# Attention steps of 16 query columns with their own key window, and the retention scores of two heads in one step

## The chip, the cores and the metric

One core of one Trainium2 chip runs the kernel. The metric is the device time of one execution in microseconds (us); below, PE is TensorE, DVE is VectorE, ACT is ScalarE, POOL is GpSimd, and SP is the engine whose queue issues most DMAs.

## What is computed

Two layers of a diffusion backbone over 256 latent tokens (a grid of 4 rows by 64 columns) and 256 context tokens, 1024 wide. Each layer is a half-step SwiGLU FFN, a mixer, and another FFN. The mixer projects the tokens once and splits the columns into three groups of heads: neighbourhood attention (A), a spatial gate (B) and bidirectional retention (C). Attention and retention, cut to what matters here:

```python
# A: 6 heads x 64. Latent query (r, c) reads all 4 grid rows, 16 columns around c, and all context keys
col_start = jnp.clip(col - NA_WIN_C // 2, 0, GRID_W - NA_WIN_C)      # WIN_C 16, GRID_W 64
s_loc = jnp.einsum('bqhd,biqjhd->bhqij', q_r, k_win) * scale + bias
s_ctx = jnp.einsum('bqhd,bchd->bhqc', q_r, kc) * scale
p = jax.nn.softmax(concatenate([s_loc, s_ctx]))
out = p_loc @ v_win + p_ctx @ vc
# C: 6 heads x 64, per direction, chunks of 128
scores = jnp.einsum('bnihd,bnjhd->bnhij', qc, kc) * intra_decay
o = scores @ vc + cross_term(state)
y = norm(o_f) * silu(g_f) + norm(o_b) * silu(g_b)
```

In layer 0 the context tokens run through the mixer too; in layer 1 only the latent tokens leave it.

## The kernel before

Every large product (FFN, input and output projection) is done three times with operands split into a high and a low part in fp32r: `product` and `product_nat` (lines 204 to 217) issue three matmuls each. The weights come in chunks of 128x1024 through `Stream`: SP loads a chunk (`_load`, line 79), ACT rounds it to the high part (`wh`, line 89), DVE subtracts for the low part (`wl`, line 100). Three chunks are loaded and up to three are split ahead of PE.

Small work is put between these products by a queue written out by hand. After each product `pump` adds `pace[0]` (times the product's width over 512) to a counter, and for each whole unit it takes the next function, a tick, from the list `bg`. A tick whose condition isn't met yet (`needs`) stays where it is. `drain_bg` empties the list. So the order on every engine is fixed when the program is built, and an engine works through its own list in that order.

The mixer (`mixer`, from line 866) runs five stretches: `nat_group` three times for q, k, v of attention and v of retention (tokens on the partitions, evacuated by `ev0`, `ev1`, `ev2`), six projections `rqk` for q and k of retention, then gate groups, the spatial gate and the output projection. Attention ticks (`na_ticks`) begin in the third `nat_group` and go on beside `rqk`; retention ticks (`ret_ticks`) follow beside the gate groups.

An attention task is a pair of heads p and an index r. For r below 4 it takes one grid row of 64 queries: `na_scores` (line 992) multiplies them with all 256 latent and 256 context keys, one matmul of 512 columns for each head, the first head in rows and output partitions 0 to 63, the other in 64 to 127. DVE adds a bias tile (256 columns of bias, in which keys outside the window are -1e30, and 256 zeros) and takes the maximum, ACT the exponent, DVE the division; `na_pt` transposes four blocks of 128 keys, ACT copies them out, `na_pv` multiplies them with four blocks of values (`vN`). For r of 4 and 5, in layer 0 alone, the context queries read the context keys. There are 12 latent tasks a layer, and 6 context tasks in layer 0. A bias tile is loaded by SP two tasks ahead.

Retention, pair p: `ret_scores(p, e, s)` (line 1240) is one head e of one stream s (latent 0, context 1; in layer 1 only the latent one): two matmuls of 64 rows by 256 columns into one PSUM bank, and four DVE products with the decay tables into `sd`. `ret_o` (line 1259) multiplies them with the values into `ro`, and adds the term of the state at the second head; then `ret_ln`, `ret_var` and `ret_gate` (norm on DVE, ACT and POOL, gates on POOL) fill `yR`, which `yt` (line 1510) transposes for the output projection. All float32 matmuls of this part go through PE in two passes, so the profile counts two for each.

Small PSUM tiles come from two banks in turn (`a_bank`), `o` and `ro` from two others (`b_bank`).

Of the kernel before, what the change touches and what calls it, by code (L numbers as in the profile page):

```python
# [9 lines left out]
F32 = mybir.dt.float32  # L10
# [6 lines left out]
D = 1024  # L17
L = 2
# [8 lines left out]
GW = 64  # L27
NEG = -1.0e30
# [30 lines left out]
RPACE = (1.2, 1.4)  # L59
# [75 lines left out]
def tile_hybrid_dit(ctx: ExitStack, tc: tile.TileContext, t_x, t_c, t_cb, t_ada0, t_ada, t_adab, t_nw, t_w1, t_w2,  # L135
# [83 lines left out]
    with tc.manual_schedule():  # L219
# [219 lines left out]
        def residual(l, i, m, ps, c0, streams):  # L439
# [185 lines left out]
        def ffn(l, f, lead, norms, steps=None, tail=None):  # L625
# [7 lines left out]
            with ExitStack() as es:  # L633
# [21 lines left out]
                for half in range(2):  # L655
# [134 lines left out]
                    for m in range(KT - 2 if split_tail else KT):  # L790
# [10 lines left out]
                        if ahead and m >= KT - 2:  # L801
                            for s in seven.prepare(JH)[slice(0, 4) if m == KT - 2 else slice(4, 7)]:
                                s()
                        residual(l, i, m, ps, 0, streams)
                        if half == 1:
# [3 lines left out]
                            if tail:  # L809
                                tail(m)  # L810
# [55 lines left out]
        def mixer(l, norms):  # L866
            last = l == L - 1
            ctx_out = not last
            with ExitStack() as es:
# [9 lines left out]
                G.memset(biasT[:, :, 256:512], 0.0)  # L879
                btasks = [(p, r) for p in range(3) for r in range(4)]  # L880

                def bias_load(i):
                    if i < len(btasks):
                        SP.dma_start(out=biasT[:, i % 3, 0:256], in_=t_bias[l, btasks[i][0], btasks[i][1]])
# [7 lines left out]
                SP.dma_start(out=sgb, in_=t_sgb[l])  # L892

# [42 lines left out]
                na = {}  # L936
# [34 lines left out]
                def qk_transpose(tt, c, dst, w):  # L971
                    def go():
                        n = dst.shape[1]
                        ps = a_bank("qkt")
                        for p in range(n):
                            PE.transpose(ps[:, 128 * p:128 * p + 128], qkn[:, tt, c + 128 * p:c + 128 * p + 128], ident)
                        S.activation(out=dst[:, :, 128 * tt:128 * tt + 128],
# [13 lines left out]

                def na_scores(p, r):
                    def go():
                        ps = a_bank("sc")
                        for e in range(2):
                            h = slice(64 * e, 64 * e + 64)
                            PE.matmul(out=ps[h], lhsT=qT[h, p, 64 * r:64 * r + 64], rhs=kT[h, p, :],
                                      start=True, stop=True)
                        sc = mp.tile([128, 512], F32, tag="sc", name="sc", bufs=3)
                        mx = mp.tile([128, 1], F32, tag="mx", name="mx", bufs=3)  # L1000
                        V.tensor_tensor_reduce(out=sc, in0=ps, in1=biasT[:, (4 * p + r) % 3], scale=1.0,
                                               scalar=-3.0e38, op0=ALU.add, op1=ALU.max, accum_out=mx)
# [27 lines left out]
                def na_divide(p, r):  # L1030
                    def go():
# [3 lines left out]
                        for b in range(n):  # L1035
                            w = 512 // n
# [810 lines left out]
```

## Time and profile before

| what | value |
|---|---|
| median of three runs | 1810.83 us (1810.07 to 1811.4) |
| the profiled execution's own time | 1812.95 us |
| its span in the trace | 1811.2 us |
| PE busy | 1778.7 us, 98% |
| PEld (weight loads) busy | 1550.2 us, 86% |
| DVE busy | 1300.8 us, 72% |
| ACT busy | 724.8 us, 40% |
| POOL busy | 260.8 us, 14% |

The span is the time from the first to the last recorded instruction; about 1.8 us of the execution lie around it. Busy time of PE counts a matmul from its start to its modelled end, and neighbours overlap, so the distance between the starts of neighbours says more than their durations. In the timeline a row is: start, duration, engine, line, operation, output and inputs, form, count, and in brackets the idle time before it with the instruction that ended it. Without brackets, the engine had not been idle.

### The profile page before, as it was taken

How to read it: one execution, taken by the hardware profiler on the slowest of the kernel's cores; microseconds unless marked ns; L12 is line 12 of the kernel's file. 1: busy time of each engine (PE TensorE's matmuls, PEld its weight loads, DVE VectorE, ACT ScalarE, POOL GpSimd, SP SyncE). 2: the span in 40 equal slices, each digit the busy share in tenths (PEclk: the TensorE clock that was granted, in tenths of full speed). 3: DMA queues.
4: the chain of work that ended last, by engine and by line, in shares of the span. 5: the costliest groups of instructions: out<-in, count | busy, mean ns of one | idle time of the engine just before them, and what ended most of it. 6: DMA issues, size and time to landing. Idle time of an engine off the chain costs nothing. (4 is left out here: it accounts for less than half of the span.)

```text
span 1811.2 us, 29366 instructions
## 1 busy us (share of the span) xinstructions
PE 1778.7 (98%) x11520; PEld 1550.2 (86%) x11520; DVE 1300.8 (72%) x2200; ACT 724.8 (40%) x1203; POOL 260.8 (14%) x307
## 2 busy tenths in 40 slices
PE   7999999999999999999999999999999999999999
PEld 5788888888668989898999898979998867899998
DVE  5789988976455566788588877776887745668665
ACT  3422222225544234452344244513542555354443
POOL 0000000002114310120222002113311104310000
PEclk9999999999999999999999999999999999999999
DMA  8656765634211122656675526567666422356654
GB/s 316 236 190 217 252 212 189 212 124 149 87 64 47 47 74 67 174 147 188 179 183 158 164 86 179 153 210 199 169 188 222 146 88 76 106 192 200 200 179 148
DMA packets 103610, 290.60 MB, mean 160 GB/s; under 512 B 12080, under 2 KB 18864, under 8 KB 103344
## 3 DMA queue, kind: packets, MB, share of 16 engines
q1 hardware_dynamic: 86192, 243.64, 41.0%
q0 software_dynamic: 17280, 45.10, 10.8%
q8 instruction: 90, 1.47, 0.3%
q14 instruction: 48, 0.39, 0.1%
HBM read 287.64 MB, written 1.05 MB: 159 GB/s over the span
## 5 line engine op out<-in xcount | busy, mean ns | idle before, releaser
L100 DVE TENSOR_TENSOR wl<-wr,wh 128x1024 fp32r<-128x1024 f32 (+2 forms) x308 | 327.0, 1087 | 112.3 <-ACT wh L89 110.9
L89 ACT CAST wh<-wr 128x1024 fp32r<-128x1024 f32 (+2 forms) x308 | 279.9, 934 | 182.2 <-PE d L207 90.5
L208 PE MATMUL d<-aTh,wl 128*128 128x512 f32 (+1 forms) x770 | 269.6, 350 | 2.0 <-DVE wl L100 2.0
L206 PE MATMUL d<-aTh,wh 128*128 128x512 f32 (+1 forms) x770 | 269.9, 351 | 1.1 <-ACT wh L89 1.1
L207 PE MATMUL d<-aTl,wh 128*128 128x512 f32 (+1 forms) x770 | 269.2, 350 | 0.0
L208 PEld LDWEIGHTS d<-aTh,wl 128*128 128x128 f32 x770 | 145.3, 189 | 24.4 <-DVE wl L100 3.2
L206 PEld LDWEIGHTS d<-aTh,wh 128*128 128x128 f32 x770 | 145.2, 189 | 22.5 <-ACT wh L89 1.3
L290 DVE CUSTOM_DVE_ANT_0 aw<-aw,cb 128x1024 f32<-128x1024 f32 x128 | 155.6, 1223 | 11.5 <-DMA aw<-in_ada_dram 8.9
L207 PEld LDWEIGHTS d<-aTl,wh 128*128 128x128 f32 x770 | 145.3, 189 | 21.1
L206 PE MATMUL g<-hTh,wh 128*128 128x512 f32 (+2 forms) x464 | 158.1, 341 | 3.0 <-ACT hTh L383 1.4
L208 PE MATMUL g<-hTh,wl 128*128 128x512 f32 (+2 forms) x464 | 156.9, 338 | 2.0 <-DVE wl L100 1.9
L207 PE MATMUL g<-hTl,wh 128*128 128x512 f32 (+2 forms) x464 | 157.1, 339 | 1.3 <-DVE hTl L366 1.1
L208 PE MATMUL u<-hTh,wl 128*128 128x512 f32 (+2 forms) x464 | 156.6, 337 | 0.4 <-DVE wl L100 0.4
L206 PE MATMUL u<-hTh,wh 128*128 128x512 f32 (+2 forms) x464 | 156.1, 336 | 0.0
L207 PE MATMUL u<-hTl,wh 128*128 128x512 f32 (+2 forms) x464 | 156.0, 336 | 0.0
L214 PE MATMUL nat<-wh,hTh 128*128 128x512 f32 (+2 forms) x384 | 136.3, 355 | 0.0
L216 PE MATMUL nat<-wh,hTl 128*128 128x512 f32 (+2 forms) x384 | 127.9, 333 | 0.4 <-DVE hTl L366 0.4
L215 PE MATMUL nat<-wl,hTh 128*128 128x512 f32 (+2 forms) x384 | 127.7, 333 | 0.0
L290 DVE CUSTOM_DVE_ANT_0 junk<-aw,cb 128x1024 f32<-128x1024 f32 x96 | 117.0, 1219 | 4.5 <-DMA aw<-in_ada_dram 4.1
L582 PE MATMUL p<-hTh,wl 128*128 128x256 f32 x408 | 116.2, 285 | 0.6
L582 PE MATMUL p<-th,wl 128*128 128x256 f32 x408 | 114.8, 281 | 0.6 <-DVE wl L551 0.5
L581 PE MATMUL p<-hTl,wh 128*128 128x256 f32 x408 | 114.6, 281 | 0.0
(262 smaller groups left out, 4044.5 us busy)
## 6 DMA issues: line engine op xcount, KB each, us to landing
wr<-in_w_dram SPq DMA_DIRECT2D x142, 512.0 KB, 4.4
aw<-in_ada_dram SPq DMA_DIRECT2D x92, 512.0 KB, 5.1
wr<-in_wi_dram SPq DMA_DIRECT2D x56, 512.0 KB, 3.6
aw<-in_ada_dram POOLq DMA_DIRECT2D x52, 512.0 KB, 4.8
wr<-in_w_dram SPq DMA_DIRECT2D x64, 384.0 KB, 3.8
wr<-in_w_dram SPq DMA_DIRECT2D x64, 320.0 KB, 3.0
q<-in_w_dram SPq DMA_DIRECT2D x68, 256.0 KB, 3.8
q<-in_w_dram POOLq DMA_DIRECT2D x68, 256.0 KB, 5.3
```

Source lines behind the costliest of these rows:

```text
L89: self.nc.scalar.copy(out=h[:, :n], in_=self.raw[i][:, :n])
L100: self.nc.vector.tensor_tensor(out=lo[:, :n], in0=t[:, :n], in1=h[:, :n].bitcast(F32), op=ALU.subtract)
L206: PE.matmul(out=ps, lhsT=wh[:, col:col + 128], rhs=hh[rhs_sl], start=start, stop=False)
L207: PE.matmul(out=ps, lhsT=wh[:, col:col + 128], rhs=hl[rhs_sl], start=False, stop=False)
L208: PE.matmul(out=ps, lhsT=wl[:, col:col + 128], rhs=hh[rhs_sl], start=False, stop=stop)
L214: PE.matmul(out=ps, lhsT=hh[lhs_sl], rhs=wh[:, wc], start=start, stop=False)
L215: PE.matmul(out=ps, lhsT=hh[lhs_sl], rhs=wl[:, wc], start=False, stop=False)
L216: PE.matmul(out=ps, lhsT=hl[lhs_sl], rhs=wh[:, wc], start=False, stop=stop)
L290: V.tensor_tensor_reduce(out=junk, in0=t, in1=cb[:, s], scale=1.0, scalar=0.0, op0=ALU.mult, op1=ALU.add, accum_out=mod[l][:, 8 * r + b, s ...
L581: PE.matmul(out=ps, lhsT=wh[:, cw], rhs=tl, start=False, stop=False)
L582: PE.matmul(out=ps, lhsT=wl[:, cw], rhs=th, start=False, stop=n == 3)
```

## The change

The latent tokens are reordered (`POS`): within a chunk of 128 tokens, two grid rows by 64 columns, the two rows of a column now stand beside each other. An attention task r is now a block of 16 grid columns with all 4 rows, again 64 queries, and its keys are the 32 grid columns from `KB0[r]` on, again with all 4 rows: 128 latent keys instead of 256. Scores have 128 + 256 columns, in two matmuls a head; transposes and values go over three blocks instead of four. The values of the four windows are gathered into `vW` by eight copies within SBUF a call (`windows`), two calls in layer 0 and three in layer 1. `vN` now lives in the tile of `yR`. The first three bias tiles are loaded at the start of the mixer and each further one behind the task three before it; the table `tab` is issued ahead of the copies.

`ret_scores(p, s)` does both heads of a pair, alternating, into the two banks of `a_bank`. The scores of the next pair stand ahead of the last gate of the pair in front. `RPACE` goes from (1.2, 1.4) to (1.3, 1.5), the ticks of `evs` stand one further apart, and `ret_weights` moves back in the list. In the last FFN the result goes through a tile `xo`, which undoes the reordering in two DVE operations of 128 columns. Tables, bias and spatial weights are permuted on the way in.

```diff
+QB, KB = 16, 32
+KB0 = (0, 8, 24, 32)
...
-RPACE = (1.2, 1.4)
+RPACE = (1.3, 1.5)
...
-        def residual(l, i, m, ps, c0, streams):
+        def residual(l, i, m, ps, c0, streams, out=None):
+
+            if out is not None:
+                for k in range(2):
+                    a, b = 128 * k, 128 * k + 128
+                    V.scalar_tensor_tensor(out=out[:, a:b].rearrange("p (r c) -> p c r", r=2),
...
-                vN = mp.tile([128, 4, 384], F32, tag="vN", name="vN")
+
+                vW = mp.tile([128, 4, 384], F32, tag="vN", name="vW")
...
                 yR = mp.tile([128, 4, 384], F32, tag="yR", name="yR")
+                vN = yR
...
+                def windows(a, b):
+
+                    for w, c0 in enumerate(KB0):
+                        for c in range(2):
+                            SP.dma_start(out=vW[64 * c:64 * c + 64, w, a:b], in_=vN[2 * c0:2 * c0 + 64, c, a:b])
...
+                for b in range(3):
+                    bias_load(b)
...
                 def na_scores(p, r):
                     def go():
                         ps = a_bank("sc")
-                        for e in range(2):
-                            h = slice(64 * e, 64 * e + 64)
-                            PE.matmul(out=ps[h], lhsT=qT[h, p, 64 * r:64 * r + 64], rhs=kT[h, p, :],
-                                      start=True, stop=True)
-                        sc = mp.tile([128, 512], F32, tag="sc", name="sc", bufs=3)
+                        kw = kT[:, p, 0:T].rearrange("p (c i) -> p c i", c=2)[:, :, 2 * KB0[r]:2 * KB0[r] + 2 * KB]
+                        for out, rhs in ((ps[:, 128:384], kT[:, p, T:NT]), (ps[:, 0:128], kw)):
+                            for e in range(2):
+                                h = slice(64 * e, 64 * e + 64)
+                                PE.matmul(out=out[h], lhsT=qT[h, p, 64 * r:64 * r + 64], rhs=rhs[h],
+                                          start=True, stop=True)
+                        sc = mp.tile([128, 512], F32, tag="sc", name="sc", bufs=3)[:, 0:384]
...
-                        for b in range(4):
+                        for b in range(3 if r < 4 else 4):
                             PE.transpose(ps[:, 128 * b:128 * b + 128], sc[:, 128 * b:128 * b + 128], ident)
...
+                            vs, nq = (vW[:, r], vN[:, 2], vN[:, 3]), 64
+                            o = o[:, 0:T].rearrange("p (c w i) -> p c w i", c=2, w=4)[:, :, r]
...
-                def ret_scores(p, e, s):
+                def ret_scores(p, s):
+
                     def go():
-                        h = 2 * p + e
-                        hp = 64 * e
                         qk = rt["qk", p]
-                        ps = a_bank("rs")
+                        pse = [a_bank("rs") for e in range(2)]
                         for b in range(2):
-                            PE.matmul(out=ps[:, 256 * b:256 * b + 256],
-                                      lhsT=qk[hp:hp + 64, 1, s * T + 128 * b:s * T + 128 * b + 128],
-                                      rhs=qk[hp:hp + 64, 0, s * T:s * T + T], start=True, stop=True)
...
+                            for e in range(2):
+                                h = slice(64 * e, 64 * e + 64)
+                                PE.matmul(out=pse[e][:, 256 * b:256 * b + 256],
+                                          lhsT=qk[h, 1, s * T + 128 * b:s * T + 128 * b + 128],
+                                          rhs=qk[h, 0, s * T:s * T + T], start=True, stop=True)
...
-                    t = []
+
+                    t = [needs(0, ret_scores(0, 0))]
                     for p in range(3):
                         k = [needs(p + 1, f(p + 1)) for f in (ret_queries, ret_keys)] if p < 2 else [nop]
+                        ahead = [needs(p + 1, ret_scores(p + 1, 0))] if p < 2 else []
                         if ctx_out:
-                            t += [needs(p, ret_scores(p, 0, 0)), ret_scores(p, 1, 0), ret_o(p, 0, 0), ret_state(p),
-                                  ret_scores(p, 0, 1), ret_o(p, 1, 0), ret_ln(p, 0), ret_scores(p, 1, 1), *k,
-                                  ret_var(p, 0), ret_o(p, 0, 1), nop, ret_o(p, 1, 1), ret_ln(p, 1), nop,
-                                  ret_var(p, 1), ret_gate(p, 0), nop, nop, ret_gate(p, 1)]
+                            t += [nop, nop, ret_o(p, 0, 0), ret_state(p), nop,
+                                  ret_o(p, 1, 0), ret_scores(p, 1), ret_ln(p, 0), nop, ret_var(p, 0), nop,
+                                  ret_o(p, 0, 1), *k, nop, ret_o(p, 1, 1), ret_ln(p, 1), ret_gate(p, 0),
+                                  ret_var(p, 1), *ahead, nop, nop, ret_gate(p, 1)]
                         else:
...
+                            t += [nop, nop, ret_o(p, 0, 0), ret_state(p), *k,
+                                  ret_o(p, 1, 0), ret_ln(p, 0), nop, ret_var(p, 0), *ahead, nop, nop, ret_gate(p, 0)]
...
                 nat_group(full, lambda tt: (0, 512), ev0, stagger=True)
+                SP.dma_start(out=tab, in_=t_tab)
+                if last:
+                    windows(0, 128)
                 bg.extend(qk_ticks(0, full))
...
-                SP.dma_start(out=tab, in_=t_tab)
                 nat_group(full, lambda tt: (384, 512) if (last and tt >= 2) else (0, 512), ev1)
+                windows(128 if last else 0, 256)
...
                 nat_group(full, lambda tt: (0, 512), ev2)
+                windows(256, 384)
```

What PE issues in layer 0 around the first value step; `nat` are the projection's matmuls, `sc` scores, `pt` transposed weights, `o` the output. Before:

```order
L1046 MATMUL pt<-ident,sc 128x128 x4
L214 MATMUL nat<-wh,hTh 128x512
L215 MATMUL nat<-wl,hTh 128x512
L216 MATMUL nat<-wh,hTl 128x512
L976 MATMUL qkt<-ident,qkn 128x128 x2
...
L997 MATMUL sc<-qkT 64x512 x2
L1066 MATMUL o<-pt,vN 64x64 x8
```

And now:

```order
L1082 MATMUL pt<-ident,sc 128x128 x3
L217 MATMUL nat<-wh,hTh 128x512
L218 MATMUL nat<-wl,hTh 128x512
L219 MATMUL nat<-wh,hTl 128x512
L1003 MATMUL qkt<-ident,qkn 128x128 x2
...
L1033 MATMUL sc<-qkT 64x256 x2
L1033 MATMUL sc<-qkT 64x128 x2
L1111 MATMUL o<-pt,vW 64x2x32 x2
L1111 MATMUL o<-pt,yR 64x2x32 x4
```

The steps stand at the same places; they have three blocks for four, and the score step has two forms.

What PE issues for the last pair of layer 1; `rs` are the retention scores (with the numbers of their tiles), `ro` the outputs, `st` the state, `sg` the spatial gate, `yt` the transposes for the output projection. Before:

```order
L1247 MATMUL rs_14998<-rqk_14551 128x256 x2
...
L1247 MATMUL rs_15012<-rqk_14551 128x256 x2
...
L1275 MATMUL ro_15030<-rv_13397,sd_15001 128x64 x6
...
L1232 MATMUL st_15040<-vw_14875,kn_14873 128x256 x2
...
L1275 MATMUL ro_15030<-rv_13397,sd_15015 128x64 x6
L1283 MATMUL ro_15030<-st_bd_13402,prep_14536 128x128 x4
...
L1513 MATMUL yt_15144<-ident_74,yR_13398 128x128 x2
```

And now:

```order
L1288 MATMUL rs_14973<-rqk_14569 128x256
L1288 MATMUL rs_14974<-rqk_14569 128x256
L1288 MATMUL rs_14973<-rqk_14569 128x256
L1288 MATMUL rs_14974<-rqk_14569 128x256
...
L1413 MATMUL sg_14992<-sgw_13408,gvu_14698 64x128 x8
...
L1318 MATMUL ro_15036<-rv_13401,sd_14979 128x64 x6
...
L1318 MATMUL ro_15036<-rv_13401,sd_14984 128x64 x6
L1326 MATMUL ro_15036<-st_bd_13406,prep_14552 128x128 x4
...
L1563 MATMUL yt_15160<-ident_74,yR_13402 128x128 x2
```

Left out are projection matmuls (and the state). Between the last scores and the first `ro` there were 9 of them, now there are 27 and the eight of the spatial gate; between the last `ro` and the first `yt` there were 39, now 48. Each is 256 columns wide.

What SP issues in layer 1, from the weight loads of the first projection on (`wr`). Before:

```order
L79 DMA wr<-in_wi_dram 128x1024 x6
L1418 DMA tab<-in_tab_dram 128x1796
L79 DMA wr<-in_wi_dram 128x1024 x4
L884 DMA biasT<-in_bias_dram 128x256 x2
L79 DMA wr<-in_wi_dram 128x1024
```

And now:

```order
L904 DMA biasT<-in_bias_dram 128x128 x3
L82 DMA wr<-in_wi_dram 128x1024 x6
L1461 DMA tab<-in_tab_dram 128x1796
L910 DMA vW<-yR 64x128 x8
L82 DMA wr<-in_wi_dram 128x1024 x4
L910 DMA vW<-yR 64x128 x8
L82 DMA wr<-in_wi_dram 128x1024
L904 DMA biasT<-in_bias_dram 128x128 x2
```

Two groups of eight copies stand between weight loads that followed each other (the table's load apart), and a third stands further on, behind the third projection.

## Rows read from the trace of the kernel before

**Rows 1.** The page, busy time of each engine over the span, share and instructions.

```profile
PE 1778.7 (98%) x11520; PEld 1550.2 (86%) x11520; DVE 1300.8 (72%) x2200; ACT 724.8 (40%) x1203; POOL 260.8 (14%) x307
```

**Rows 2.** Windows of layer 0: us, then busy (instructions) by engine, PEclk, DMA share, GB/s.

```profile
457.00:483.00 26.00, 26.00 (x156) 16.86 (x158) 13.29 (x37) 11.67 (x24) 0.67 (x1) 1.00 0.25 81
555.00:600.00 45.00, 45.00 (x327) 40.41 (x325) 24.60 (x56) 14.13 (x29) 18.68 (x23) 1.00 0.16 48
```

**Rows 3.** Timeline of PE at one score step: start us, us, line, out<-in, forms, count.

```profile
456.33 0.39 PE L215 MATMUL nat<-wl,hTh 128*128 128x512 f32 x1
456.56 0.39 PE L216 MATMUL nat<-wh,hTl 128*128 128x512 f32 x1
456.88 1.07 PE L997 MATMUL sc<-qkT 64*64 64x512 f32 x4
...
458.46 0.40 PE L216 MATMUL nat<-wh,hTl 128*128 128x512 f32 x1
```

**Rows 4.** Timeline of PE at one transpose step, layer 0.

```profile
466.63 0.39 PE L216 MATMUL nat<-wh,hTl 128*128 128x512 f32 x1
466.87 0.60 PE L1046 MATMUL pt<-ident,sc 128*128 128x128 f32 x4
...
467.77 0.39 PE L216 MATMUL nat<-wh,hTl 128*128 128x512 f32 x1
```

**Rows 5.** Timeline of PE, a context score step and the value step behind it.

```profile
478.07 1.08 PE L1017 MATMUL sc<-qkT 64*64 64x256 f32 x8
479.08 0.69 PE L1066 MATMUL o<-pt,vN 128*64 128x64 f32 x16
```

**Rows 6.** Tile sc: duration of one pass, ns min/median/max, first and last start.

```profile
L997 PE MATMUL sc<-qkT x96: 589/614/641, 456.9 to 1508.3; 64*64 64x512 f32 x96
...
L1017 PE MATMUL sc<-qkT x48: 376/376/427, 478.1 to 541.1; 64*64 64x256 f32 x48
```

**Rows 7.** Timeline of PE at one retention score step of one head.

```profile
557.68 0.28 PE L215 MATMUL nat<-wl,hTh 128*128 128x256 f32 x1
557.80 0.28 PE L216 MATMUL nat<-wh,hTl 128*128 128x256 f32 x1
558.01 1.13 PE L1247 MATMUL rs<-rqk 64*128 64x256 f32 x4
...
559.41 0.28 PE L216 MATMUL nat<-wh,hTl 128*128 128x256 f32 x1
```

**Rows 8.** Timeline of PE, line 1275 undisturbed, and held in layer 0 and 1.

```profile
561.50 1.45 PE L1275 MATMUL ro<-rv,sd 128*128 128x64 f32 x12
...
612.24 1.83 PE L1275 MATMUL ro<-rv,sd 128*128 128x64 f32 x12 [0.66 <-DVE sd L1252]
...
1569.37 1.88 PE L1275 MATMUL ro<-rv,sd 128*128 128x64 f32 x12 [1.01 <-DVE sd L1252]
```

**Rows 9.** Window behind the last of these, columns as in rows 2.

```profile
1571.01:1574.42 3.41, 3.41 (x14) 3.05 (x14) 0.09 (x1) 0.57 (x3) 0.19 (x1) 0.50 0.00 0
```

**Rows 10.** Timeline of PE, the last transpose of the retention output, layer 1.

```profile
1587.12 0.44 PE L1513 MATMUL yt<-ident,yR 128*128 128x128 f32 x2 [2.52 <-POOL yR L1304]
```

**Rows 11.** DMA issues: tile, queue, count, KB each, median us to landing.

```profile
wr<-in_wi_dram SPq DMA_DIRECT2D x56, 512.0 KB, 3.6
...
tab<-in_tab_dram SPq DMA_DIRECT2D x2, 898.0 KB, 6.9
```

**Rows 12.** Timeline of SP and ACT in layer 1, around the table load.

```profile
1432.55 0.42 SPq L1418 DMA_DIRECT2D tab<-in_tab_dram  x1
1435.91 13.10 SPq L79 DMA_DIRECT2D wr<-in_wi_dram  x4
...
1446.36 1.04 ACT L89 CAST wh<-wr 128x1024 fp32r<-128x1024 f32 x1
```

**Rows 13.** Tile sd: a 128-column VectorE operation out of PSUM, ns.

```profile
L1253 DVE TENSOR_TENSOR sd<-rs,prep x18: 271/278/281, 559.5 to 1570.3; 128x128 f32<-128x128 f32 x18
```

**Rows 14.** Timeline of VectorE, the last residual of the run.

```profile
1807.62 0.48 DVE L441 SCALAR_TENSOR_TENSOR xT<-d,mod,xT 128x256 f32<-128x256 f32 x1 [2.90 <-PE d L208]
```

More of the change, by code (lines that the diff above doesn't have):

```diff
@@ L803, in ffn @@
                                 s()
+                        if tail and half == 1:
+                            o = fp.tile([128, T], F32, tag="xo", name="xo", bufs=4)
+                            residual(l, i, m, ps, 0, streams, o)
+                            tail(m, o)
+                            continue
                         residual(l, i, m, ps, 0, streams)
@@ L976, in go @@
                             PE.transpose(ps[:, 128 * p:128 * p + 128], qkn[:, tt, c + 128 * p:c + 128 * p + 128], ident)
+                        if w == 0 and tt < 2:
+                            S.activation(out=dst[:, :, 0:T].rearrange("p b (w c i) -> p b w c i", w=4, c=2)[:, :, :, tt],
+                                         in_=ps[:, 0:128 * n].rearrange("p (b w i) -> p b w i", b=n, w=4),
+                                         func=AF.Copy, scale=qkw[:, l, w:w + 1])
+                            return
                         S.activation(out=dst[:, :, 128 * tt:128 * tt + 128],
@@ L1048, in go @@
                         if r < 4:
-                            S.copy(out=pt, in_=ps)
+                            S.copy(out=pt[:, 0:384], in_=ps[:, 0:384])
                         else:
@@ L1090, in na_ticks @@
                     n = len(tasks)
-                    nb = [0]
+                    nb = [3]
                     def next_bias():
@@ L1742, in _tables @@
     sin = (np.sin(a) * np.where(d % 32 < 16, -1.0, 1.0)[:, None]).astype(f32)
[L1743 to L1744 removed]
+    sw = np.concatenate([128 + POS, POS])
+    dif = POS[None, :] - POS[:, None]
     df = np.concatenate([128 + dif, np.maximum(dif, 0)], 1)
@@ L1798, in _layout @@
     r["qkw"] = np.concatenate([qk, qk], 1).transpose(1, 0, 2)
-    bias = np.full((L, 3, 4, 2, GW, 4, GW), NEG, f32)
+    bias = np.full((L, 3, 4, 2, 2, QB, 2, 2, KB, 2), NEG, f32)
     col = np.arange(GW)
@@ L1806, in _layout @@
             for cq in range(GW):
+                w, c = divmod(cq, QB)
                 ck = np.arange(start[cq], start[cq] + WIN_C)
-                bias[:, :, r_, :, cq, kr, ck[0]:ck[-1] + 1] = rpb[:, :, :, kr - r_ + 7, ck - cq + WIN_C - 1]
-    r["bias"] = bias.reshape(L, 3, 4, 128, 256)
-    r["sgw"] = sg_w.transpose(0, 3, 1, 2)
-    r["sgb"] = np.repeat(sg_b.reshape(L, 2, 2, 128).transpose(0, 2, 1, 3), 64, axis=1)
+                bias[:, :, w, :, r_ // 2, c, r_ % 2, kr // 2, ck[0] - KB0[w]:ck[-1] + 1 - KB0[w], kr % 2] = (
+                    rpb[:, :, :, kr - r_ + 7, ck - cq + WIN_C - 1])
+    r["bias"] = bias.reshape(L, 3, 4, 128, 128)
+    r["sgw"] = sg_w[:, :, POS][:, :, :, POS].transpose(0, 3, 1, 2)
+    r["sgb"] = np.repeat(sg_b[:, :, POS].reshape(L, 2, 2, 128).transpose(0, 2, 1, 3), 64, axis=1)
     ln = np.stack([sg_ln_w, sg_ln_b], 1)
```

78 lines of the change are left out of this document (41 added, 37 removed).

## The prediction

> **What bounds the kernel now.** I read the page first, then windows, then the timeline of TensorE step by step. The page shows PE busy 1778.7 us of 1811.2, against 1300.8 on VectorE and 724.8 on ScalarE [rows 1]. A busy PE need not be at its peak, so the windows: while layer 0 does attention, PE has no idle time at all in 26 us, and VectorE and ScalarE are busy for only half of it; the same in its retention stage, 45.00 of 45.00 [rows 2]. So an instruction taken off PE there is time taken off the end, unless something new makes PE wait. What a small step costs is not its own duration but how far it pushes the projection matmuls apart. Between two neighbours of 512 columns lie 0.23 us, and 1.90 between 456.56 and 458.46 with one score step and two more neighbours between: the step costs 1.90 - 3 x 0.23 = 1.21 us [rows 3]. This is how I price every step.
>
> **Attention, 24 latent steps (12 a layer).** Each loses 128 of its 512 key columns. A 512-column pass lasts at least 589 ns, a 256-column pass 376, so a column is worth (589 - 376) / 256 = 0.83 ns; the two heads go side by side and float32 takes two passes, so 128 columns are 2 x 128 x 0.83 = 0.21 us [rows 6]. The step becomes eight instructions instead of four. That costs nothing: the context step has eight of 256 columns in 1.08 us, the same column count as the four of 512 in 1.07 [rows 3, 5]. Four transposes push the neighbours 1.14 - 0.69 = 0.45 us apart; one fewer saves 0.11 [rows 4]. Sixteen value passes take 0.69 us, of which I put down a third to entry and drain (the last pass of a context step, 0.376, is a third of that step's 1.08), so four fewer save 0.12; the ends are 0 and 4 x 0.69 / 16 = 0.17 [rows 5, 6]. Together 0.44 us, times 24 = **10.6 us**. The shorter maximum, exponent, divide and copy on VectorE and ScalarE run beside PE and count nothing.
>
> The two heads of a score step write halves of one PSUM bank, and the eight passes still fit into 1.08 us [rows 5]. The Trainium skill, TensorEngine Tiling (Array Packing), Restrictions and Gotchas, says that different row tiles cannot access the same bank at the same time; by that rule the heads would go one after the other, the column saving would double and the total would be 5 us lower. Here the trace differs from it, so I give it no chance.
>
> **Retention scores, 18 head steps become 9.** One head's step has four passes of 256 columns and costs 1.61 - 3 x 0.12 = 1.25 us [rows 7]. The four do not overlap: four take 1.13 us where eight paired ones of the same column count take 1.08 [rows 5, 7]. The change alternates the heads, which sit in the lower and the upper 64 rows of the array and go to two banks. No row of before shows that form (64 rows, all 128 output columns). The bounds are 1.20, a paired step that is no worse than attention's, and 1.25 + 4 x 0.25 = 2.25, no overlap at all, 0.25 being (1.13 - 0.376) / 3 a pass [rows 6, 7]. The nearest row is the paired one of 256 columns in float32, and I take 1.25: 18 x 1.25 - 9 x 1.25 = **11.3 us**.
>
> **Waits that go.** In the last pair of each layer the products of the scores (ro) waited for VectorE: 0.66 us and then 1.83 instead of 1.45 in layer 0, 1.01 and then 1.88 in layer 1, so 1.0 and 1.4 us [rows 8]. Behind the second the granted clock was 0.50 for 3.41 us, the 1.2 GHz level, which costs up to half of that, 1.7 us [rows 9]. Before, nine projection matmuls (1.06 us) lie in front of that ro in layer 1; in the new order 27 of them and the gating matmuls do, over 3.2 us, while VectorE needs four products of 0.28 to 0.42 us for a head [rows 13]. I take both waits as gone: **4.1 us**. The wait of the last transpose, 2.52 us, is for a chain (norm, POOL gate) that starts at the last ro; the new order puts nine more matmuls of 0.118 in between: **1.1 us** less, 1.4 stay [rows 10].
>
> **What it adds.** Five groups of eight copies within SBUF stand on SP's queue with weight loads behind them. The issue of a DMA takes 0.42 us, a group 3.4; in layer 1 the first group follows the table, which takes 6.9 us to land [rows 11, 12]. If the last copy waited for that, the load now issued at 1435.91 would leave at 1439.9. It lands 3.6 us later, at 1443.5, and its cast on ScalarE runs at 1446.36: covered, with 2.9 us left [rows 11, 12]. Were that cover gone, ScalarE's evacuations behind the cast would be late and PE with them. Between a group and the first value step that reads it stand over 6 us of projection matmuls and three attention steps in the new order, against 3.4 us of issue and 3.6 of landing. The last residual becomes two 128-column operations, 2 x 0.28 against 0.48: **+0.1 us** at the very end [rows 13, 14]. The bias loads move forward by less than a step; RPACE only spreads the queue of steps; both cost nothing while VectorE and ScalarE are half idle. With PE faster, one of nine joint steps may find VectorE late: I allow one wait of the size of the two above, **+1.2 us**.
>
> **Sum.** -10.6 - 11.3 - 4.1 - 1.1 + 0.1 + 1.2 = -25.8 us. Against the profiled execution, 1812.95, that gives 1787.2; the median of the three runs is 1810.83, 2.1 lower, so **1785.0 us**.
>
> **Rivals.** *A: the heads do not run side by side.* For it: no row shows this form; against it: float32 pairs in 64-row halves do in attention [rows 5]. A joint step then costs 2.25, the nine save 2.3 instead of 11.3, and the time is 1794.0. Between the ends it falls in between. (The Trainium skill, TensorE: Matmul & The Clock Gate, Part 3, measured 3.07x for four row tiles, 77% of the ideal; an estimate by that share stretches the paired passes from 1.0 to 1.3 us and gives 1787.7; no row here shows it.) *B: PE meets new waits in attention.* Steps come 0.44 us sooner, and the chain maximum, exponent, divide, transpose does not shrink as much. If half of the 24 steps give their gain back, 1790.3; all, 1795.6. Against it: VectorE and ScalarE are half idle there [rows 2]. *C, slower: SP holds the weights.* If the copies land one by one, a group holds SP for 8 x 3.6 = 29 us; the cover is 1446.36 - 1439.5 = 6.9 us, so five groups cost 5 x 22 = 110 us: 1895. It decides from 6.9 us a group on, and the kernel is slower than before from 12.8 (6.9 + 29.4 / 5). Against it: the load behind the table left 3.4 us after it, long before it landed [rows 11, 12].
>
> **Chances.** Forecast 0.78, A 0.11, B 0.08, C 0.03. The forecast's own range is 1780.5 (no wait returns, the last transpose's wait and the slow clock behind it go, 4.4 us lower) to 1788. The range reaches to A's end: 1780.5 to 1794. About 0.2% (3.6 us) is what a measurement of this kernel can tell from no change: faster 0.96, same 0.01, slower 0.03.
>
> **What would show it.** Score steps of eight passes that cost 1.0 us; three transposes at 0.33; joint retention steps of eight passes within about 1.1 us, starts in pairs (two more passes' worth each, and A is right); no ro row with a VectorE wait of 1 us in the last pair; one slow-clock stretch fewer; about 1.4 us before the last transpose. Wrong would be casts on ScalarE waiting for weight loads behind the copies (C), or transposes waiting for VectorE or ScalarE (B).

## The result, and the profile after

The median of four runs is 1793.32 us (1792.47 to 1796.28), against 1810.72 for the kernel before on the same chip: the ratio is 0.990, with a 95% interval of 0.9884 to 0.9915. The forecast was 1785.0 with a range of 1780.5 to 1794.0, so the direction held and the time lies just inside the upper end; the forecast's own range, without the rivals, ended at 1788. The profiled execution took 1793.33 us (span 1791.6), 19.6 less than that of before, where the sum said 25.8: 6.2 us of the miss of 8.3. The other 2.1 is the difference between before's profile (1812.95) and its median, which the profile after does not have.

The page, busy time by engine, answers to [rows 1]:

```profile
PE 1755.4 (98%) x11496; PEld 1544.3 (86%) x11496; DVE 1294.0 (72%) x2208; ACT 719.1 (40%) x1203; POOL 257.1 (14%) x307
```

PE lost 23 us of busy time and is still busy for 98% of the span. To see where the time went, the span is cut at the first product of each stage (`nat`, `su`, `op`, the next FFN), which stands at the same place in every kernel here. "Attention" runs from the first `nat` to the first gate group, "retention" from there to `op` (with `su`), "projection" to the FFN behind the mixer. All in us, from one profile each:

| kernel | L0 attention | L0 retention | L0 projection | L1 attention | L1 retention | L1 projection |
|---|---|---|---|---|---|---|
| before | 146.02 | 96.10 | 49.40 | 126.37 | 47.08 | 27.47 |
| after | 142.13 | 87.15 | 50.39 | 122.00 | 46.29 | 25.27 |
| e1, sg bank | 142.16 | 87.15 | 49.43 | 122.08 | 40.26 | 26.77 |
| e2, heads in turn | 142.17 | 87.19 | 50.37 | 122.01 | 46.15 | 25.27 |
| e3, attention alone | 142.09 | 96.13 | 49.40 | 121.35 | 47.09 | 27.46 |
| e4, retention alone | 145.99 | 87.14 | 50.38 | 126.98 | 46.47 | 26.78 |
| e5, copies twice | 142.11 | 87.15 | 50.38 | 126.88 | 46.38 | 26.76 |
| e6, weights back | 140.83 | 87.14 | 50.38 | 122.02 | 45.36 | 26.77 |
| e7, spacing back | 142.12 | 87.15 | 50.38 | 122.08 | 42.10 | 26.78 |
| e9, three edits | 140.84 | 87.14 | 49.42 | 121.98 | 40.27 | 25.22 |
| e11, gate later | 140.83 | 87.14 | 49.42 | 122.01 | 40.27 | 24.07 |
| e10, three tiles | 140.78 | 87.14 | 49.42 | 121.98 | 40.27 | 23.60 |

Stages with the same code agree within about 0.1 us from run to run, far better than the whole: the stretch ahead of the first mixer alone varies from 405.1 to 410.5 us, though no edit touches it. The exceptions are the last two columns, where a stretch at the lower clock comes or not: layer 1's retention takes 45.36 us in e6, with the granted clock at 0.50 for 3.41 us, and 46.29 in the change, with 6.83 us of it; for the projection see the last section. So the stages, read together with the clock, and not the medians, decide differences of a microsecond. From before to after the six columns sum to -19.2 us; the stretches outside them give -0.4.

**What came as forecast.** Timeline of PE in layer 0, a score step and a transpose step (start us, us, line, forms, count); answers to [rows 3, 4]:

```profile
454.88 0.40 PE L219 MATMUL nat<-wh,hTl 128*128 128x512 f32 x1
455.21 0.87 PE L1033 MATMUL sc<-qkT 64*64 64x256 f32 x8
...
456.57 0.39 PE L219 MATMUL nat<-wh,hTl 128*128 128x512 f32 x1
...
464.34 0.39 PE L219 MATMUL nat<-wh,hTl 128*128 128x512 f32 x1
464.57 0.49 PE L1082 MATMUL pt<-ident,sc 128*128 128x128 f32 x3
...
465.37 0.39 PE L219 MATMUL nat<-wh,hTl 128*128 128x512 f32 x1
```

By the reckoning of the prediction the score step costs 456.57 - 454.88 - 3 x 0.23 = 1.00 us (1.21 before), and the three transposes 465.37 - 464.34 - 3 x 0.23 = 0.34 (0.45 before).

Groups of instructions by line in the retention stage of layer 0, before (L1247) and after (L1288): busy us, mean ns of one, idle time ahead of it.

```profile
L1247 PE MATMUL rs<-rqk 64*128 64x256 f32 x48 | 13.5, 402 | 0.0
```

```profile
L1288 PE MATMUL rs<-rqk 64*128 64x256 f32 x48 | 6.8, 402 | 0.0
```

The same 48 passes of the same length cover half the time: they run two at a time.

**What did not.** Timeline of PE and VectorE in layer 1, from the last joint score step to the spatial gate's products `sg` (in brackets the idle time before, and what ended it):

```profile
1541.47 0.28 PE L219 MATMUL nat<-wh,hTl 128*128 128x256 f32 x1
1541.68 1.13 PE L1288 MATMUL rs<-rqk 64*128 64x256 f32 x8
...
1542.08 0.88 DVE L878 TENSOR_TENSOR gvu<-gvu,r 128x512 f32<-128x512 f32 x1 [0.24 <-POOL r L875]
...
1543.09 0.28 PE L219 MATMUL nat<-wh,hTl 128*128 128x256 f32 x1
...
1543.74 1.27 DVE L103 TENSOR_TENSOR wl<-wr,wh 128x1024 fp32r<-128x1024 f32 x1 [0.78 <-ACT wh L92]
...
1545.73 0.41 DVE L1294 TENSOR_TENSOR sd<-rs,prep 128x256 f32<-128x256 f32 x1
...
1546.46 0.41 DVE L1298 TENSOR_TENSOR sd<-rs,prep 128x256 f32<-128x256 f32 x1
...
1546.92 1.97 PE L1413 MATMUL sg<-sgw,gvu 128*64 128x128 f32 x16 [3.55 <-DVE sd L1298]
```

The joint step itself costs 1543.09 - 1541.47 - 3 x 0.118 = 1.27 us, as forecast. But `sg`'s operand `gvu` was written at 1542.96 and PE stood until 1546.9, until VectorE had finished the four products of the first head. `sg` reads nothing of those. What it shares with them is PSUM: it draws its bank from the pair of `a_bank`, and the joint step has just taken both. From 1545.56 on, still within the stall, the clock was at the 1.2 GHz level for 6.83 us (window of that stretch, columns as in [rows 2]):

```profile
1545.56:1552.39 6.83, 5.47 (x32) 5.14 (x33) 3.80 (x13) 0.55 (x1) 3.39 (x3) 0.50 0.23 77
```

Smaller waits, in the same view: the first value step of layer 0 with the VectorE and ScalarE work in front of it, `sg` of layer 0 with the `yt` whose bank it draws again and VectorE's reads of `yt`, the first `ro` of layer 1, and the last transpose, which answers to [rows 10]:

```profile
484.36 0.62 DVE L1185 TENSOR_SCALAR ww<-lg,tab 128x6 f32<-128x6 f32 x4
...
485.01 0.22 ACT L1187 ACTIVATE ww<-ww 128x24 f32<-128x24 f32 x1 [1.83 <-DVE ww L1185]
...
486.46 0.49 ACT L1085 COPY pt<-pt 128x384 f32<-128x384 f32 x1
...
487.00 0.34 PE L1111 MATMUL o<-pt,vW 128*64 128x64 f32 x4 [1.26 <-ACT pt L1085]
...
634.86 0.60 PE L1563 MATMUL yt<-ident,yR 128*128 128x128 f32 x4
...
639.47 1.40 DVE L1566 SCALAR_TENSOR_TENSOR hTl<-yt,gnw,hTh 128x512 fp32r<-128x512 f32 x2
...
640.27 1.09 PE L1413 MATMUL sg<-sgw,v 128*64 128x128 f32 x16 [0.89 <-DVE hTl L1566]
...
1509.04 1.83 PE L1318 MATMUL ro<-rv,sd 128*128 128x64 f32 x12 [0.21 <-DVE sd L1294]
...
1569.43 0.44 PE L1563 MATMUL yt<-ident,yR 128*128 128x128 f32 x2 [1.82 <-POOL yR L1347]
```

SP and ScalarE in layer 1 around the first group of copies, answers to [rows 12]; ahead of it the copies' own row from the view of tile `vW` (ns min/median/max of one issue):

```profile
L910 SPq DMA_DIRECT2D vW<-yR x40: 462/594/752, 450.5 to 1479.4; - x40
```

```profile
1420.69 0.42 SPq L1461 DMA_DIRECT2D tab<-in_tab_dram  x1
1421.16 8.11 SPq L910 DMA_DIRECT2D vW<-yR  x8
1429.37 7.78 SPq L82 DMA_DIRECT2D wr<-in_wi_dram  x4
...
1434.50 1.04 ACT L92 CAST wh<-wr 128x1024 fp32r<-128x1024 f32 x1
```

A group held SP for 8.1 us, not 3.4. Seven of its copies were issued at up to 0.75 us each by 1425.7; the eighth was issued at 1428.79, 0.02 us after the table had landed (8.1 us behind its issue at 1420.69). In the trace's records that copy waits for semaphore 104, the one that tells of the table's landing: the DMAs around the table take eight semaphores in turn, and the copy is the eighth behind it. The pause of 3.1 us is the case that the prediction named ("If the last copy waited for that"). The cast behind it ran at 1434.50; in the kernel before it ran at 1446.36, and this stage began 11.84 us later there (1408.56 against 1396.72), so it is not late at all.

### The profile page after: what moved, and what is told of

The parts are those of the page before. It is cut to its first block, busy times and chain, and to the rows that moved or that the text cites. A ratio compares the mean times of both kernels' runs of the same rounds, so it can differ in the third digit from the quotient of the medians.

```text
span 1791.6 us, 29394 instructions
## 1 busy us (share of the span) xinstructions
PE 1755.4 (98%) x11496; PEld 1544.3 (86%) x11496; DVE 1294.0 (72%) x2208; ACT 719.1 (40%) x1203; POOL 257.1 (14%) x307
```

## The experiments

**e1. A bank from the other pair for `sg`.**

```diff
                     def sg_mix(s):
...
-                        ps = a_bank("sg")
+                        ps = b_bank("sg")
```

> The changed kernel with one word altered: the spatial gate's products (sg) take their PSUM bank from the pair that ro and o use, not from the pair of which the joint retention scores now hold both. Bank theory: in layer 1 sg waited 3.55 us for the scores' products on VectorE to free a bank, though its operand was ready at 1542.96. It then starts at about 1543.2, the stretch of half clock behind it goes, and so does the wait of about 1 us in layer 0: sg falls from 5.88 and 2.19 us of displacement to 1.2 each, and the projection matmuls behind it lose their 1.5 us at half clock. Total 6 to 7 us less, about 1786.5. Rival, VectorE theory: it is VectorE that is late there, whatever the bank; then the first ro behind waits instead (sd is written at 1545.7 to 1547.9) and the total falls by less than 3 us, 1790 or more. Second rival, the operand: sg waits just as before, 1793.

Measured: 1787.99 us (1787.05 to 1788.43), ratio 0.987 (0.9855 to 0.9885). Timeline of PE and VectorE in layer 1 at the same place, and the last transpose; then the window behind that transpose:

```profile
1542.95 1.09 PE L1413 MATMUL sg<-sgw,gvu 128*64 128x128 f32 x16
...
1545.41 0.42 DVE L1294 TENSOR_TENSOR sd<-rs,prep 128x256 f32<-128x256 f32 x1
...
1546.94 1.45 PE L1318 MATMUL ro<-rv,sd 128*128 128x64 f32 x12
...
1563.05 0.44 PE L1563 MATMUL yt<-ident,yR 128*128 128x128 f32 x2 [1.83 <-POOL yR L1347]
```

```profile
1563.94:1567.35 3.41, 3.41 (x19) 3.41 (x18) 0.48 (x1) 0.99 (x2) 0.00 (x0) 0.50 0.02 5
```

`sg` now starts 2.5 us before VectorE touches the scores, with no wait, and the `ro` behind it has none either. The bank theory holds: layer 1's retention stage falls by 6.03 us and layer 0's projection by 0.96. (In layer 0 it is not a joint step that holds the bank: `sg` draws the bank of the first `yt`, 634.86, and VectorE read that `yt` only from 639.47 on.) VectorE is as late as before, only nobody needs it. The other 1.5 us went back: now the clock fell behind the last transpose, where in the change, with the same wait of 1.82 us, it had not.

**e2. The two heads in turn.**

```diff
-                        for b in range(2):
-                            for e in range(2):
+                        for e in range(2):
+                            for b in range(2):
```

> The changed kernel, where the joint retention step issues the four matmuls in the order head 0, head 0, head 1, head 1 and no longer in alternation; banks, products and order of steps are the same. If the saving comes from neighbours on different row halves that run side by side, only the passes at the change of head overlap: a joint step costs 2.0 to 2.25 us instead of 1.26, nine of them 6.7 to 9 us more, 1800 to 1802. If it comes from having one step instead of two (one entry and one drain of the queue instead of two), a step still costs about 1.26 and the time stays at 1793.

Measured: 1794.11 us (1790.11 to 1794.6), every stage as in the change. The order of issue did change; the order of one such step in the changed kernel and here, `rs_4728` and `rs_4729` being the two heads' banks:

```
-L1288 MATMUL rs_4728<-rqk_4165 128x256
-L1288 MATMUL rs_4729<-rqk_4165 128x256
-L1288 MATMUL rs_4728<-rqk_4165 128x256
-L1288 MATMUL rs_4729<-rqk_4165 128x256
+L1288 MATMUL rs_4728<-rqk_4165 128x256 x2
+L1288 MATMUL rs_4729<-rqk_4165 128x256 x2
```

Timeline of PE at that step, and a window of the first 0.1 us of it, `rs` alone (us, PE busy, passes in it, PEclk, DMA); then the same window at a one-head step of the kernel before:

```profile
1542.62 1.14 PE L1288 MATMUL rs<-rqk 64*128 64x256 f32 x8
```

```profile
1542.60:1542.70 0.10, 0.08 (x2) 1.00 0.69 246
```

```profile
1563.98:1564.08 0.10, 0.08 (x1) 1.00 0.59 246
```

The time fits the rival that expects about 1.26 us, but its reason does not: two passes are running in the first 0.1 us, although four of head 0 were issued ahead of the first of head 1. The halves run side by side, and they do so without being alternated. My first theory had the mechanism right and its condition wrong.

**e3 and e4. Each half alone.** e3 is the changed kernel with `ret_scores`, `ret_ticks`, RPACE and the spacing of before; e4 is the kernel before with those four of the change.

```diff
-RPACE = (1.3, 1.5)
+RPACE = (1.2, 1.4)
...
-                def ret_scores(p, s):
+                def ret_scores(p, e, s):
...
-                            at = min(at + 3, len(bg))
+                            at = min(at + 2, len(bg))
```

> The attention half of the change alone: scores per head, the retention steps' order, RPACE and the spatial gate's spacing are those of before. If the parts add up, 24 steps save 10.5 us, the wait of 1.3 us at the first value step of layer 0 stays, and the waits of ro and yt of before are back: 1801.5 us (1800 to 1803). If attention gives its gain back in new waits (the rival B of the prediction), 1806 or more.

> The retention half of the change alone, in the kernel before: joint scores, the new order of the retention steps, RPACE and the spacing of the spatial gate's steps. If the parts add up, 11.2 us less for the nine joint steps, about 4 less for the waits of ro that go, and about 7 more for the spatial gate that waits for a bank and the half clock behind it: 1802 to 1803. If the wait of the spatial gate is only there because the attention steps run ahead of VectorE, sg doesn't wait here and the time is 1796.

Measured: e3 1803.19 us (1801.47 to 1803.71), ratio 0.9953 (0.9938 to 0.9968); e4 1803.01 (1798.77 to 1805.47), ratio 0.9946 (0.9925 to 0.9966), both beside 1811.39 for before. That is -8.2 and -8.4, together -16.6 against -17.4 for the change: the halves add up. By the stages of the table they give 8.9 and 8.7 us, the change 19.2; 1.5 of the difference is the slow stretch in the last stage, which e4 has and the change has not. PE in layer 1 of e3 at the `ro` that waited in [rows 8], and `sg` in layer 1 of e4:

```profile
1559.04 1.83 PE L1315 MATMUL ro<-rv,sd 128*128 128x64 f32 x12 [1.02 <-DVE sd L1292]
```

```profile
1557.75 1.98 PE L1373 MATMUL sg<-sgw,gvu 128*64 128x128 f32 x16 [3.58 <-DVE sd L1258]
```

e3 keeps the old wait (1.02 us against 1.01); e4 has the new one, without any attention step running ahead. So the wait of `sg` belongs to the retention half alone.

**e5. Every copy twice.**

```diff
-                    for w, c0 in enumerate(KB0):
+                    for w, c0 in [*enumerate(KB0)] * 2:
```

> The changed kernel, where each of the five calls of windows issues its eight copies twice; nothing else. In the changed kernel a group holds the SP queue for 4.9 to 8.1 us in layer 1, more than the 3.4 of the prediction, and PE shows no wait behind one. If the cover was as wide as the prediction said (about 3 us past the first group), 5 to 8 us more of issue in each group uses it up in layer 1: the weight casts behind the groups start late and PE waits there, 1 to 4 us in all, 1794 to 1797. If the copies' transfers weigh on the other loads too (rival C), more than 10 us. If nothing on SP is near its edge, 1793.

Measured: 1798.79 us (1797.39 to 1802.05). Only layer 1's attention stage changed, by 4.88 us. SP, ScalarE and PE there:

```profile
1420.84 12.66 SPq L910 DMA_DIRECT2D vW<-yR  x16
1433.59 7.08 SPq L82 DMA_DIRECT2D wr<-in_wi_dram  x4
...
1438.01 1.04 ACT L92 CAST wh<-wr 128x1024 fp32r<-128x1024 f32 x1 [3.74 <-PE nat L218]
...
1440.20 0.50 PE L217 MATMUL nat<-wh,hTh 128*128 128x512 f32 x1 [2.15 <-ACT yR L959]
```

Counted from the start of the stage (1396.37 here, 1396.72 in the change), the load left 4.6 us later and landed 5.0 later (1437.91 against 1433.23). Its cast ran 0.10 us behind the landing, which ended its wait, and not the matmul that the bracket names; it ran 3.9 later than in the change. PE stood 2.15 us, was then 2.3 us later than in the change, and ran at half clock for 6.83 us (1441.11 to 1447.94). So the change had 1.2 us left between landing and cast and some 1.5 more at PE. Rival C is a real mechanism and begins between 8.1 and 12.7 us of hold for this group; at 12.7 it costs 4.9 us.

**e6. `ret_weights` at the head of the list again.**

```diff
-                t.insert(DEC[l][1], ret_weights)
...
-                bg.extend(t + ret_ticks())
+                bg.extend([ret_weights] + t + ret_ticks())
```

> The changed kernel with ret_weights back at the head of the list of steps, as before, and no longer in the sixth place of layer 0. If its four VectorE operations and ScalarE's exponent, which waited for them from 483.2 to 485.0, are what made the copy of the transposed weights late, the wait of 1.3 us at the first value step of layer 0 (487.00) shrinks to under 0.4 and the time falls by 1 us, to 1792. If the decay tables' exponents and the evacuations that stand there too make the copy late, the wait stays over 1 us and the time at 1793.

Measured: 1794.03 us (1792.32 to 1794.88), no gain that the medians show. The stage shows it: layer 0's attention is 1.30 us shorter than in the change. ScalarE and PE at the first value step:

```profile
488.96 0.50 ACT L1085 COPY pt<-pt 128x384 f32<-128x384 f32 x1
489.57 0.20 PEld L1111 LDWEIGHTS o<-pt,vW 128*64 128x64 f32 x4 [0.17 <-ACT pt L1085]
```

The copy comes 1.3 us after its transposes (487.65) where it came 2.7 after them (483.75) in the change. The cause is the four VectorE operations that ScalarE waited for. In this profile the stretches ahead of the mixer took 3.9 us more, and the slow clock behind the last transpose, which the change did not have, cost 1.5; both hide the gain in the total.

**e7. The spatial gate's steps two apart again.**

```diff
-                            at = min(at + 3, len(bg))
+                            at = min(at + 2, len(bg))
```

> The changed kernel with the spatial gate's steps two apart again, as before, in place of three. In layer 1 its products then stand 15 projection matmuls ahead of the last joint score step, where in the change they stand three behind it. By the bank theory the wait for the scores' products goes (VectorE's products come later than sg); sg may wait for its own norm instead, since its chain has 6 us less: up to 2 us. Total 3 to 6 us less in layer 1, about 1788 to 1790. If VectorE is simply overloaded there, the wait moves to sg's operand or to the next ro and the time stays above 1791.

Measured: 1789.98 us (1788.29 to 1790.69), ratio 0.988 (0.9852 to 0.9907). PE in layer 1:

```profile
1538.83 1.09 PE L1413 MATMUL sg<-sgw,gvu 128*64 128x128 f32 x16 [0.56 <-DVE gvu L878]
...
1546.69 1.83 PE L1318 MATMUL ro<-rv,sd 128*128 128x64 f32 x12 [0.70 <-DVE sd L1294]
```

With `sg` ahead of the joint step the 3.55 us are gone without another bank. It waits 0.56 for its own norm, and the `ro` 1.08 us in all (0.70 of idle and 0.38 more in its own duration, 1.83 against 1.45): 4.2 of e1's 6.0 us. The change's own move of `sg`, three apart instead of two, is what put it behind the joint step.

**e9, e11, e10. Towards a better version.** e9 takes e1 and e6 and, in layer 1, the last retention part last:

```diff
-                KORD = (0, 1, 2, 5, 6, 7, 3, 4)
+                KORD = (0, 1, 2, 5, 6, 3, 4, 7) if last else (0, 1, 2, 5, 6, 7, 3, 4)
...
-                for m in range(nm, 3):
-                    yt(m + 5)
+                if not last:
+                    for m in range(nm, 3):
+                        yt(m + 5)
                 for kt in KORD[3:6]:
+                    if kt == 3:
+                        yt(7)
```

> The changed kernel with the bank of the first experiment, ret_weights back at the head, and in layer 1 the last part of the retention output taken last: the output projection takes its inputs in the order 0, 1, 2, 5, 6, 3, 4, 7, and the last transpose (yt) stands 12 projection matmuls later. The wait of 2.0 us at yt falls to about 0.6, since 12 matmuls of 0.118 us stand in front of it now, and the stretch of half clock that the first experiment still had behind it goes (1.5 us). With the 5.3 us of the bank and 1 us of the weights: 1784 to 1785. If the products behind yt wait for its evacuation or for the spatial gate's split instead, 1786 to 1788.

Measured: 1786.24 us (1785.41 to 1787.13), ratio 0.9858 (0.9835 to 0.9881). The transpose no longer waits and no slow stretch follows, but the products that read the parts in front wait (the second case of the expectation). VectorE, ScalarE and PE there:

```profile
1560.63 0.69 DVE L1426 TENSOR_TENSOR gvu<-gvu 128x512 f32<-128x512 f32 x1
...
1561.35 0.62 ACT L1556 CAST hTh<-gvu 128x512 fp32r<-128x512 f32 x1 [1.67 <-DVE gvu L1426]
...
1561.87 0.83 ACT L1564 ACTIVATE hTh<-yt,gnw 128x256 fp32r<-128x256 f32 x2
...
1562.39 0.38 PE L209 MATMUL op<-hTh,wh 128*128 128x256 f32 x1 [0.57 <-ACT hTh L1564]
```

The evacuation of `yt` stood on ScalarE behind the gate's cast, which waited 1.67 us for VectorE. e11 issues the gate behind the first two transposes; e10 is e11 with three output tiles at a time.

```diff
-                if last:
-                    sg_gate(0)
                 nm = NM[l]
...
-                    if m < 3:
+                    if m < (2 if last else 3):
                         yt(m + 5)
+                    if last and m == 1:
+                        sg_gate(0)
```

```diff
-NM = (4, 2)
+NM = (4, 3)
```

> The kernel before this one (bank, ret_weights at the head, last retention part last) with the spatial gate's product and split (sg_gate) issued behind the first two transposes yt and no longer ahead of them. In that kernel the two matmuls behind the second yt waited 1.5 us, because the yt evacuation on ScalarE stood behind the split, which waited for VectorE. That wait goes; PE then reaches the last yt 1.5 us sooner, and its gate on POOL ends at about 1563.6 of that trace, so about 0.6 to 1 us of it comes back as a wait there: 1785.3 to 1785.7. If the split now comes too late for inputs 3 and 4, PE waits there instead and nothing is gained: 1786.2 or more.

> The same, with three output tiles of the projection in work instead of two in layer 1 (NM 3), which puts 24 more than the 21 projection matmuls of the other between the second and the last transpose less what they replace (36 against 21, 1.8 us). The last wait of the retention output is then covered altogether: 1784.5 to 1785. If three tiles need a third weight chunk before ScalarE and VectorE have split it, PE waits for that: 1786 to 1787.

Measured: e11 1783.97 us (1783.29 to 1785.01), ratio 0.9848 (0.9827 to 0.9869); e10 1785.85 (1784.51 to 1787.41), ratio 0.9857 (0.9831 to 0.9883). e11's projection stage is 1.15 us shorter than e9's; the wait at the last transpose, of which 0.6 to 1 us was expected back, did not come back. e10's stage is another 0.47 shorter. That e10's profile is 2.8 us longer than e11's all the same (span 1785.2 against 1782.4) does not come from its edit: the stretch ahead of the first mixer took 4.0 us more, and the clock was at the 1.2 GHz level in the first FFN, where e11's was at the 2.4 GHz level in the same window:

```profile
25.26:32.09 6.83, 6.83 (x46) 4.78 (x46) 3.99 (x9) 2.55 (x4) 0.00 (x0) 0.50 0.62 239
```

e11 beats both kernels: 27 us less than before, 9 less than the change (1784.0 against 1793.3). Of e10 against e11 the stages say 0.5 us better; the medians (1785.85 against 1783.97) do not show it, and only one execution of each is profiled, so it stays open.

## Why the prediction was right, and where it fell short

- **Attention, 10.6 us: right.** The score step fell by 0.21 and the transposes by 0.11, as put down. By stages, e6 shows 5.2 us in layer 0 (146.02 to 140.83) and e3 5.0 in layer 1 (126.37 to 121.35): 10.2 together, which leaves 0.10 for a value step where 0.12 was taken. This takes the whole difference for the steps; layer 0 has a new wait of 0.2 us at a context score step in it (535.86).
- **Retention pairing, 11.3 us: right in size.** Nine joint steps of 1.26 us for eighteen of 1.25 are 11.2 us. The value taken (1.25, between 1.20 and 2.25) by the nearest row was the right choice, and rival A is excluded. The reason given, that the heads alternate, is not needed (e2). The Trainium skill, TensorE: Matmul & The Clock Gate, Part 3 (the estimate of 1787.7 by its 3.07x), would have made the paired passes a third longer by that estimate; the trace has them at 376 ns as a single head's, 216 ns from pair to pair.
- **Waits that go, 4.1 us: right.** In e1, where nothing else disturbs the stage, layer 1's retention is 6.82 us shorter; the four head steps that stood in it and are one joint step now account for 3.7, which leaves 3.1 for the wait (1.4) and its slow clock (1.7). In layer 0, 8.95 less 7.4 (twelve head steps that are six) leaves 1.5 where 1.0 was put down; the other 0.5 was not traced. Whether the new order, RPACE or the joint step removed these waits was not separated: e4 has all three.
- **The last transpose, 1.1 us: 0.7.** Its wait fell from 2.52 to 1.82, and e1, with the clock falling as it did before, has a projection stage 0.70 shorter. What took the other 0.4 was not traced.
- **The step that failed is the allowance "one wait of the size of the two above, +1.2".** Measured are 1.3 us at the first value step of layer 0 (e6), 1.0 at `sg` in layer 0 and 6.0 at `sg` in layer 1 with its slow clock (e1), and 0.7 at a `ro` in layer 1 (122.00 us of attention stage against 121.35 in e3): 9.0, less 1.5 because no slow clock followed the last transpose. That is 7.5 where 1.2 stood: 6.3 too little, where the whole sum was short by 6.2 (the misses of the other terms cancel but for 0.1). The wait was looked for at the wrong instruction: the prediction expected it at a `ro` that finds VectorE late, and of that came 0.7 us. In layer 1 it is the next user of the bank pair that waits, a step that reads none of the scores, since a joint step holds both banks until VectorE has emptied one. The diff said so (in `ret_scores`, two draws from `a_bank` in one step), and in the order of layer 1 `sg` stood three matmuls behind it. In layer 0 `sg` waits in the same way, but for the bank of a `yt`; what made VectorE later there was not found, and the spacing alone is not it (50.38 us with the old one in e7). The move of `ret_weights` the prediction did not price at all, and it calls VectorE and ScalarE "half idle": it cost 1.3 us (e6), since ScalarE works in order and a copy that PE needed stood behind it.
- **That the range held is luck.** The forecast's own range ended at 1788. The part above it was there for rival A, slow joint steps, and these did not come; other waits filled it. And the 1.5 us of slow clock behind the last transpose, which the sum had kept, were missing in the profile of the change for a reason that is open; with them the time would be near 1794.8 by these figures (an estimate), outside the range.
- The Trainium skill, Perfetto Trace Analysis, Optimizing Tensor Performance, Matmuls, wants independent matmul groups to go through different PSUM banks, so that the evacuation of one overlaps the next group. The traces agree: 1.09 us for `sg` with a free bank (e1), 1.97 at the 1.2 GHz level behind 3.55 of idle time without.
- **Rival B** (new waits in attention): one value step waits over 1 us, for `ret_weights` and not because steps come sooner (e6), and one score step 0.2 us. **Rival C**: not reached, but the prediction's figures were off. A copy's issue took 0.59 us (median) where 0.42 was put down, and the eighth copy went out only when the table had landed, so the group took 8.1 us instead of 3.4. The threshold of 6.9 us was passed without a wait; e5 puts it between 8.1 and 12.7.
- **The tail, +0.1**: the last residual lasts 0.69 us against 0.48 [rows 14], but the stretch behind the second mixer varies between 200.9 and 202.1 us where its code is the same, so this term can't be told from nothing.

## What to carry to other kernels

When a step takes two buffers of a rotating pair at once, look not at the step but at the next one that draws from the pair: it now waits for the whole evacuation of the first buffer, and everything queued ahead of that on the evacuating engine. Ask of every moved small step on a half-idle engine what stands behind it in that engine's order and who waits for that; the share of idle time is no cover. Where the whole varies by more than the effect, cut the profile into stages that start at the same instruction, and compare those.

## What the runs showed of the hardware that was not expected

- **Matmuls in the two row halves did not need to be issued alternately.** In e2 four passes of head 0 (two matmuls of two passes) stand ahead of head 1's, and still two passes run from the first 0.1 us on, 13 ns apart in the trace's records, where in the kernel before the second pass of one head starts 0.32 us after the first. The joint step costs 1.27 us against 1.26 alternated. The records don't name the head. That the pairs are of different heads is concluded from the kernel before, where passes of one head never overlap so, and from the semaphores in the records: in the pair at 1542.62 the second pass waits for one of its own (103, the first for 109), as in the change at 1541.69, while the second matmul of one head, into the same bank, has no wait in the kernel before. The Trainium skill, TensorE: Matmul & The Clock Gate, Part 3, The mechanism, has matmuls start strictly in program order, with only weight loads pulled ahead; by this conclusion the run differs from it.
- **The price of one slow-clock stretch.** In the traces the projection stage of layer 1 is 26.76 to 26.78 us in five kernels in which the clock stood at 1.2 GHz for 3.41 us behind the last transpose (e1, e4 to e7), and 25.27 in the two in which it did not (the change and e2), with the same wait of 1.8 us: 1.50 us. Why it fell in the one and not in the other is open.
- **Copies within SBUF of 32 and 64 KB cost SP 0.46 to 0.75 us of issue each** in the change, where the loads ahead of them had taken 0.43 or less. The group behind the table load held the queue for 8.1 us, because its eighth copy takes the table's semaphore again and is issued only when the table has landed: 0.02 us behind the landing in all ten kernels that have these copies (1428.79 in the change, 1427.90 in e5).
